# Fewer weight units split ahead at the norm boundaries of a two-layer encoder, and later loads for the first Strassen tile

## The chip, the cores and the metric

The kernel runs on one core of a Trainium2 chip. The metric is device time in microseconds (us) from one launch of the kernel; lower is better. The compute engines are TensorE (PE, with its weight loads shown as PEld), VectorE (DVE), ScalarE (ACT) and GpSimd (POOL). SyncE (SP) and POOL issue the transfers.

## The reference

Two sequences, one of 512 tokens (the prompt) and one of 256 (the sample), pass through two layers of a bidirectional encoder with 1024 features. Each layer has three parts, and each part ends in a layer norm:

```python
for l in range(DEPTH):                                   # DEPTH = 2
    mod = (silu(c) @ ada_w[l] + ada_b[l]).reshape(B, 9, D_MODEL)
    h = modulate(x, mod[:, 0], mod[:, 1])
    x = layer_norm(ALPHA * x + 0.5 * (1 + mod[:, 2]) * swiglu(h, ffn1_wi[l], ffn1_wo[l]), ...)
    h = modulate(x, mod[:, 3], mod[:, 4])
    o = concat([rms_norm(window_attention(h @ w_in)), rms_norm(hyena(h @ w_in))]) @ w_out[l]
    x = layer_norm(ALPHA * x + (1 + mod[:, 5]) * o, ...)
    h = modulate(x, mod[:, 6], mod[:, 7])
    x = layer_norm(ALPHA * x + 0.5 * (1 + mod[:, 8]) * swiglu(h, ffn2_wi[l], ffn2_wo[l]), ...)
```

`swiglu(h)` is `(silu(g) * u) @ wo` with `g, u = split(h @ wi)`; the inner width is 2816, 22 tiles of 128.

## The kernel before, in words

All 768 tokens are held with features on the partitions, so the activations are eight tiles of 128 features by 768 tokens (columns 0 to 511 are the prompt, 512 to 767 the sample). Every operand of a product is split into a high and a low part (type fp32r) and each product is three matmuls: high by high, high by low, low by high.

**Weight units.** Weights stand in DRAM as `w_units`, blocks of 128 by 1024 numbers (512 KB). A unit is loaded by SP into a raw buffer (`slot_r`, seven of them), then split: ACT copies it to the high half of a `slot_w` buffer (six of them), and DVE subtracts to make the low half. `w_ahead(n)` splits units, in the order in which they are used, until n are ready beyond those taken; `w_take()` hands out the next one; `w_load` issues the raw loads up to three units past the one just split. `w_state["limit"]` ends the run of units at the head of a feed-forward part, which has six of them.

**The order.** The schedule is written out by hand: every engine carries out its instructions in the order in which the Python code issues them, and waits on the data of others. So what stands earlier in the code on ACT or DVE delays what stands later on the same engine.

**A norm boundary.** `final` ends a part and begins the next one; there are five such boundaries (feed-forward to mixer, mixer to feed-forward, feed-forward to feed-forward, and again the first two in layer 1). It first does the sample's output products (`sample_out`). Then a loop over eight output tiles d does the prompt's products on PE, and beside it the layer norm of the sample: `norm.stats(1)`, `norm.bcast(1)`, and `norm.apply(1, i)`, which normalises one tile, modulates it and splits it into `hh` and `hl`, the inputs of the next part. Inside this loop, and once after it, `w_ahead` splits units for the next part. Then `proj.head` runs:

- for each of n_head units (six ahead of a feed-forward part, four ahead of a mixer) it takes the unit, calls `w_ahead`, does 24 matmuls of 256 sample columns, and calls `hook(i)`;
- `hook(0)` makes the statistics of the prompt (`norm.stats(0)`: eight PE transposes, DVE reductions, a power on POOL) and calls `proj.early()`;
- `hook(2)` broadcasts them (`norm.bcast(0)`, eight PE transposes) and issues `norm.apply(0, d)` for all eight prompt tiles in one go;
- after the units comes the prompt's loop: four units by eight input tiles by three matmuls of 512 columns, then `mid()`, the activations of those four, `late()`, and the last two units on the prompt.

Here the six units of the head are called u0 to u5. A unit's split has the form `slot_w<-slot_r 128x1024` in the profile, on ACT and on DVE.

**The first Strassen tile.** In a feed-forward part tiles 0 to 2 (six units) use the plain product, and the other 19 tiles use a Strassen product of seven half-size products (class `Fast`). The first of them, tile 3 (`NHEAD`), needs two raw units, loaded by `load(NHEAD, slot_r)`. Its sums and splits are made in `late()`. `mixed(d)` makes sums of activations for it on DVE and ACT. Four of the seven `slot_r` buffers hold joined activations (`full(d)` for d over 3) from the sample's `norm.apply` on until `mixed` is done.

Of the kernel before, what the change touches and what calls it, by code (L numbers as in the profile page):

```python
# [152 lines left out]
@with_exitstack  # L153
def encoder_kernel(ctx, tc, *args):
    ctx.enter_context(tc.manual_schedule())
    last = {}
    _program(_Memory(None, None, None, SLOTS, last), None, *args)
    _program(_Memory(tc.nc, tc, ctx, SLOTS, last), tc.nc, *args)


def _program(mem, nc, x_in, c_col, c_row, w_units, ada_nat, ada_t, ada_b, ln_p, conv_p, sink_in, grp_in,
# [4 lines left out]
    def slot_s(shape, dtype=F32):  # L166
        return mem.alloc("slot_s", shape, dtype)

    def slot_w(shape, dtype=F32R):
        return mem.alloc("slot_w", shape, dtype)  # L170
# [6 lines left out]
    def slot_t(shape, dtype=F32):  # L177
        return mem.alloc("slot_t", shape, dtype)
# [9 lines left out]
    def f32(ap):  # L188
        return ap.bitcast(F32)

    def tt(out, a, b, op, eng=vec):
        eng.tensor_tensor(out=out, in0=a, in1=b, op=op)
# [10 lines left out]
    def acopy(out, a):  # L203
        act.activation(out=out, in_=a, func=AF.Copy)
# [27 lines left out]
    n_units = len(w_order)  # L232
# [3 lines left out]
    def w_load(upto):  # L236
        while w_state["dma"] < min(upto, w_state["limit"]):
            i = w_state["dma"]
            w_raw[i] = slot_r([D])
            sp.dma_start(w_raw[i], w_units[w_order[i]])  # L240
            w_state["dma"] += 1

    def w_ahead(n):
        while w_state["split"] < min(w_state["next"] + n, w_state["limit"]):
            i = w_state["split"]
            w_load(i + 1)
            raw = w_raw.pop(i)
            w = slot_w([2, D])
            acopy(w[:, 0], raw)
            tt(w[:, 1], raw, f32(w[:, 0]), ALU.subtract)  # L250
            w_split[i] = w
            w_state["split"] += 1
            w_load(i + w_state["raws"])
# [13 lines left out]
    def pump(n):  # L267
        while n > 0 and background:
            try:
                next(background[0])  # L270
            except StopIteration:
                background.pop(0)
                continue
            n -= 1

    def drain():
        while background:
            pump(1)
# [35 lines left out]
    def split_to(hi, lo, src):  # L314
        acopy(hi, src)
        tt(lo, src, f32(hi), ALU.subtract)
# [88 lines left out]
    def coef_of(l, mod, c0):  # L405
        c = tiny([ND, 2])
        ts(c, mods[l][:, mod], c0, c0)
        return c
# [26 lines left out]
    class Proj:  # L435
# [15 lines left out]
            self.done(i, 0, bp[:, :LP])  # L451
            self.done(i, 1, bs[:, :LS])

        def early(self):
            pass

        mid = late = early

        def head(self, n, hook):

# [58 lines left out]
    def out_add(o, coef, d):  # L519

        bp, bs = bank(), bank()
        o.d([(bp[:, :LP], 0), (bs[:, :LS], 1)], d)
        v = slot_t([T])
        for s, b in ((0, bp[:, :LP]), (1, bs[:, :LS])):
            act.activation(out=v[:, SEQ[s]], in_=b, func=AF.Copy, scale=coef[:, d, s:s + 1])
        gp.dma_start(x_spill[:, d, :], v, accum_op=ALU.add)

    def sample_out(os, norm):

        for o in os:  # L530
            for i in range(4):
                if i in o.hooks:
                    o.hooks[i]()
                outs = []
                for j in range(2):
                    b, more = o.place(1, 2 * i + j, j == 1)
                    o.d([(b, 1)], 2 * i + j, more=more)
                    outs.append(b)
                for j in range(2):
                    if o is os[-1]:  # L540
                        norm.add(2 * i + j, 1, outs[j])
                    else:
                        norm.plain(2 * i + j, 1, outs[j])
                pump(1)
        drain()

    def final(os, norm, proj, n_head, spill):

        sample_out(os, norm)
        o = os[-1]  # L550
        n_units = sum(o.n for o in os)
        when = (0, 2, 3) if n_units > 4 else (1, 3, 4)
        for d in range(ND):
            bp, more = o.place(0, d)
            for i, part in enumerate(os):
                part.d([(bp, 0)], d, more=more or i > 0, less=part is not o)
            w_ahead(min(4, 6 - n_units + sum((d + 1) * part.n // 8 for part in os)))
            if d == when[0]:
                norm.stats(1)
            if d == when[1]:  # L560
                norm.bcast(1)
            for i in range(2 * (d - when[2]), 2 * (d - when[2]) + 2):
                if 0 <= i < ND:
                    norm.apply(1, i)
            norm.add(d, 0, bp)
        for i in range(2 * (ND - when[2]), ND):
            norm.apply(1, i)
        for j in range(2):
            spill(1, j)
        norm.low()  # L570
        norm.low()
        norm.squares()
        w_ahead(6)

        def hook(i):
            if i == 0:
                norm.stats(0)
            elif i == 2:
                norm.bcast(0)
                for d in range(ND):  # L580
                    norm.apply(0, d)
                    if d % 4 == 3:
                        spill(0, d // 4)
                norm.low()
                norm.low()
            if i == 0:
                proj.early()

        proj.head(n_head, hook)

    def results(os, norm):
# [24 lines left out]
    def swiglu(x, hh, hl, l, which):  # L616
        a_tiles, pend = {}, {}

        def a_of(j):
            if j // 2 not in a_tiles:  # L620
                a_tiles[j // 2] = slot_s([2, 2, T], F32R)
            return a_tiles[j // 2][:, j % 2]

        def done(i, s, ps):
            j, c = i // 2, SEQ[s]
            if i % 2 == 0:
                if (j, 0) not in pend and (j, 1) not in pend:
                    pend[j] = slot_t([T])
                act.activation(out=pend[j][:, c], in_=ps, func=AF.Silu)
                pend[(j, s)] = True  # L630
                return
            sg, a = pend[j], a_of(j)
            tt(sg[:, c], sg[:, c], ps, ALU.mult)
            pend[("d", j)] = pend.get(("d", j), 0) + 1
            split_to(a[:, 0, c], a[:, 1, c], sg[:, c])

        proj = Proj(hh, hl, done)
        fast = Fast(hh, hl, w_fast[2 * l + which // 2], a_of, which)
        proj.fast, proj.early, proj.mid, proj.late = fast, fast.early, fast.mid, fast.late

        def rest(end):
            coef = None
            os = []
            fast.begin()
            for ci, chunk in enumerate(CHUNKS):
                last = ci + 1 == len(CHUNKS)
                while fast.j < UNTIL[ci]:
                    fast.period(fast.j + 1 == UNTIL[ci])
                if coef is None:
                    coef = coef_of(l, 3 * which + 2, 0.5 / ALPHA)  # L650
                o = Out([(a_of(j)[:, 0], a_of(j)[:, 1]) for j in chunk])
                if ci + 2 >= len(CHUNKS):
                    if not os:
                        xn = Feat()
                        for i in range(2):
                            gp.dma_start(xn.more(i), x_spill[:, 4 * i:4 * i + 4, :])
                    o.room = 6 - sum(before.n for before in os)
                    os.append(o)
                    if last:
                        drain()  # L660
                        return end(os, xn, coef)
                    continue
                w_state["limit"], o.ahead = w_state["next"] + len(chunk), 1
                for d in range(ND):
                    out_add(o, coef, d)
                    pump(1)
                    if d % 2:
                        w_ahead(2)

        return proj, rest  # L670

    class Fast:
# [25 lines left out]
            al = slice(0, T)  # L698
            tt(self.full(d, al), f32(self.hh(d, al)), f32(self.hl(d, al)), ALU.add)

        def early(self):
            self.load(NHEAD, slot_r)

        def mid(self):
            for d in range(4):
                self.mixed(d)

# [458 lines left out]
    def first_h(d):  # L1166
        for c, s in ((SEQ[0], 0), (SEQ[1], 1)):
# [6 lines left out]
            tt(h[1](d, c), v, f32(h[0](d, c)), ALU.subtract, eng=vec if s else gp)  # L1174

    part = swiglu(x, *h, 0, 0)
    hs = [lambda d=d: first_h(d) for d in range(ND)]
    filt[1].spectra(0, sides(hs[0], hs[1], hs[2], skip, hs[3], skip, hs[4], skip))
# [581 lines left out]
    for i in range(len(PARTS)):  # L1760
# [5 lines left out]
        part = part[1](lambda os, xx, coef, i=i: finish(i, os, xx, coef))  # L1766
# [159 lines left out]
```

## Time and profile before

| | |
|---|---|
| median of 3 runs | 2939.13 us (2938.8 to 2939.33) |
| the profiled execution | 2938.19 us, span 2936.2 us |
| PE busy | 2837.5 us, 97% of the span |
| DVE, ACT, POOL busy | 2139.2 us, 1367.5 us, 331.8 us |
| mean granted TensorE clock | 0.987 |
| DMA, mean over the span | 124 GB/s |

The span runs from the first to the last instruction of the profiled execution; its own time is 1.99 us longer and 0.94 us under the median of the runs. PE is busy nearly all the time, so the time changes where PE idles or where its clock falls. A timeline row gives the start in us, the duration in us of the merged instructions, the engine, line (always that of a helper that records every call), operation, output and inputs by tile name, shapes, how many instructions were merged, and in brackets the idle time of that engine just before and what ended it.

### The profile page before, as it was taken

The page shows a single profiled execution, that of the slowest core. Times are in us where ns is not written, and L with a number is a line of the kernel's source. Part 1 is how long each engine was busy: PE and PEld are TensorE (multiplying, and loading weights), DVE is VectorE, ACT ScalarE, POOL GpSimd, SP SyncE. Part 2 cuts the span into 40 slices and gives each one's busy share as a digit, 9 for nine tenths or more (in the row PEclk, how much of TensorE's full clock was granted, in tenths as well). Part 3 has the DMA queues.
Part 4 walks back from the last instruction along what each step waited for, and adds up shares of the span by engine and source line. Part 5 has one row for each costly group of instructions (what it writes and reads, how often), then busy time and mean ns, then how long its engine had stood idle before and what let it go on. Part 6 is the DMA issues. An engine that isn't in the chain of part 4 may idle for free. (4 is left out here: it accounts for less than half of the span.)

```text
span 2936.2 us, 42164 instructions
## 1 busy us (share of the span) xinstructions
PE 2837.5 (97%) x16468; PEld 2594.4 (88%) x16468; DVE 2139.2 (73%) x3821; ACT 1367.5 (47%) x2355; POOL 331.8 (11%) x394
## 2 busy tenths in 40 slices
PE   9999999999998999999999999999999899999998
PEld 3789999988887889999988999998888788999997
DVE  5788778878967887777588777557896787444558
ACT  3544444444366544444445444444436644444444
POOL 2400000031000300000030000002100030000000
PEclk9999999999999999999999999999999999999999
DMA  5546665542121135664333665344212112455332
GB/s 202 194 171 173 188 176 164 147 151 103 57 73 51 65 127 161 194 194 116 107 122 122 179 176 157 107 107 145 102 63 73 51 57 89 85 115 115 97 108 83
DMA packets 102607, 364.65 MB, mean 124 GB/s; under 512 B 13750, under 2 KB 17031, under 8 KB 99208
## 3 DMA queue, kind: packets, MB, share of 16 engines
q1 hardware_dynamic: 74968, 259.88, 24.5%
q0 software_dynamic: 27440, 102.08, 16.2%
q8 instruction: 129, 2.11, 0.3%
q14 instruction: 70, 0.57, 0.1%
HBM read 284.33 MB, written 80.74 MB: 124 GB/s over the span
## 5 line engine op out<-in xcount | busy, mean ns | idle before, releaser
L70 PE MATMUL bank<-slot_s,slot_w 128*128 128x384 f32 (+2 forms) x13176 | 2322.1, 336 | 44.0 <-DVE slot_s L70 26.7
L70 PEld LDWEIGHTS bank<-slot_s,slot_w 128*128 128x128 f32 x13176 | 2130.5, 190 | 212.2 <-DVE slot_s L70 23.0
L70 DVE TENSOR_TENSOR slot_w<-slot_w,slot_w 128x1024 fp32r<-128x1024 f32 (+2 forms) x444 | 370.0, 864 | 4.1 <-ACT slot_w L70 1.6
L70 DVE CUSTOM_DVE_ANT_0 slot_t<-slot_r,slot_r 128x1024 bf16<-128x1024 f32 x256 | 311.4, 1223 | 77.4 <-DMA x_spill<-slot_t 45.0
L70 ACT ACTIVATE slot_w<-slot_w 128x1024 fp32r<-128x1024 f32 (+1 forms) x298 | 249.7, 838 | 119.2 <-DVE slot_w L70 118.9
L70 DVE TENSOR_TENSOR slot_w<-slot_r,slot_w 128x1024 fp32r<-128x1024 f32 (+1 forms) x194 | 222.0, 1153 | 113.4 <-ACT slot_w L70 111.9
L70 ACT ACTIVATE slot_t<-bank,tiny 128x512 f32<-128x512 f32 (+1 forms) x256 | 147.5, 580 | 307.9 <-PE bank L70 302.1
L70 POOL DMA_DIRECT2D x_spill<-slot_t x128 | 110.4, 862 | 1409.2 <-ACT slot_t L70 1409.2
L70 ACT ACTIVATE slot_w<-slot_r 128x1024 fp32r<-128x1024 f32 (+1 forms) x194 | 189.0, 992 | 155.9 <-DVE slot_r L70 98.1
L70 ACT ACTIVATE slot_t<-slot_t 128x384 f32<-128x384 f32 (+2 forms) x161 | 84.1, 526 | 334.2 <-DVE slot_t L70 334.0
L70 DVE TENSOR_TENSOR slot_t<-bank,slot_t 128x384 f32<-128x384 f32 x228 | 125.5, 555 | 144.2 <-PE bank L70 73.5
L70 DVE TENSOR_TENSOR slot_s<-slot_t,slot_s 128x768 fp32r<-128x768 f32 (+2 forms) x190 | 153.1, 810 | 52.6 <-ACT slot_s L70 48.4
L70 ACT ACTIVATE slot_s<-slot_t 128x768 fp32r<-128x768 f32 (+2 forms) x160 | 113.8, 717 | 159.9 <-DVE slot_t L70 155.5
L70 ACT ACTIVATE slot_t<-bank 128x384 f32<-128x384 f32 (+3 forms) x282 | 139.6, 495 | 101.6 <-PE bank L70 99.1
L70 PE MATMUL bank<-slot_s,slot_r 128*128 128x384 f32 x912 | 172.0, 337 | 0.0
L70 PEld LDWEIGHTS bank<-slot_s,slot_r 128*128 128x128 f32 x912 | 160.6, 188 | 0.0
L70 DVE TENSOR_TENSOR slot_r<-slot_w,slot_r 128x512 fp32r<-128x512 f32 x76 | 52.0, 684 | 106.4 <-ACT slot_r L70 106.4
L70 ACT ACTIVATE slot_t<-slot_s 128x256 f32<-128x256 f32 (+1 forms) x132 | 65.9, 510 | 108.0 <-DVE slot_s L70 104.1
L70 PE MATMUL bank<-slot_w,slot_s 128*128 128x256 f32 x864 | 107.9, 284 | 3.1 <-DVE slot_w L70 1.8
L70 PEld LDWEIGHTS bank<-slot_w,slot_s 128*128 128x128 f32 x864 | 104.7, 191 | 3.9 <-DVE slot_w L70 2.1
L70 DVE SCALAR_TENSOR_TENSOR slot_t<-bank,slot_t 128x384 f32<-128x384 f32 x76 | 42.3, 556 | 83.4 <-PE bank L70 82.2
L70 DVE SCALAR_TENSOR_TENSOR slot_s<-bank,tiny,slot_s 128x256 f32<-128x256 f32 (+1 forms) x160 | 87.0, 564 | 15.1 <-PE bank L70 14.9
(137 smaller groups left out, 2132.2 us busy)
## 6 DMA issues: line engine op xcount, KB each, us to landing
slot_r<-w_units SPq DMA_DIRECT2D x170, 512.0 KB, 4.8
slot_w<-w_units SPq DMA_DIRECT2D x146, 512.0 KB, 4.1
slot_r<-ada_t SPq DMA_DIRECT2D x128, 512.0 KB, 5.8
x_spill<-slot_t POOLq DMA_DIRECT2D x128, 384.0 KB, 5.3
slot_s<-x_spill POOLq DMA_DIRECT2D x12, 1536.0 KB, 8.2
x_spill<-slot_s POOLq DMA_DIRECT2D x10, 1024.0 KB, 4.6
slot_r<-ada_nat SPq DMA_DIRECT2D x16, 512.0 KB, 5.9
g_main<-slot_s POOLq DMA_DIRECT2D x4, 1536.0 KB, 10.0
```

The lines of the kernel that those rows point to most:

```text
L70: return getattr(real, name)(*args, **kwargs)
```

## The change

Inside the loop of `final` at most two units are split ahead instead of four, and the call after the loop also asks for two instead of six. `hook(0)` no longer calls `early`; the loads that `early` issued now stand at the start of `mid`, after the prompt's loop.

```diff
@@ class Proj
-        def early(self):
+        def mid(self):
             pass
 
-        mid = late = early
+        late = mid
@@ final
-            w_ahead(min(4, 6 - n_units + sum((d + 1) * part.n // 8 for part in os)))
+            w_ahead(min(2, 6 - n_units + sum((d + 1) * part.n // 8 for part in os)))
...
         norm.squares()
-        w_ahead(6)
+        w_ahead(2)
@@ hook in final
-            if i == 0:
-                proj.early()
-
@@ swiglu
-        proj.fast, proj.early, proj.mid, proj.late = fast, fast.early, fast.mid, fast.late
+        proj.fast, proj.mid, proj.late = fast, fast.mid, fast.late
@@ class Fast
-        def early(self):
+        def mid(self):
             self.load(NHEAD, slot_r)
-
-        def mid(self):
             for d in range(4):
                 self.mixed(d)
```

The calls in `Proj.head` stay as they are: `w_ahead(min(2, 6 - len(ws)))` after each `w_take()`.

## Rows read from the trace of the kernel before

**Rows 1.** The page, busy time of each engine, share of the span, instructions.

```profile
PE 2837.5 (97%) x16468; PEld 2594.4 (88%) x16468; DVE 2139.2 (73%) x3821; ACT 1367.5 (47%) x2355; POOL 331.8 (11%) x394
```

**Rows 2.** Windows: start:end, length, busy us (instructions) by engine, PEclk, DMA share, GB/s.

```profile
960.00:1050.00 90.00, 84.15 (x456) 72.92 (x456) 76.71 (x136) 45.15 (x72) 30.68 (x33) 0.94 0.16 59
1050.00:1470.00 420.00, 416.75 (x2371) 397.09 (x2370) 310.33 (x470) 184.90 (x296) 28.70 (x34) 1.00 0.54 154
```

**Rows 3.** Timeline of PE, boundary from mixer to feed-forward, layer 0.

```profile
983.67 11.98 PE L70 MATMUL bank<-slot_s,slot_w 128*128 128x512 f32 x55
...
1000.06 2.00 PE L70 MATMUL bank<-slot_s,slot_w 128*128 128x256 f32 x6 [2.39 <-DVE slot_s L70]
1004.07 1.44 PE L70 MATMUL bank<-slot_s,slot_w 128*128 128x256 f32 x5 [2.00 <-DVE slot_s L70]
1005.31 1.91 PE L70 MATMUL bank<-ident,slot_t 128*128 128x128 f32 x8
1006.87 6.96 PE L70 MATMUL bank<-slot_s,slot_w 128*128 128x256 f32 x48
...
1014.46 46.06 PE L70 MATMUL bank<-slot_s,slot_w 128*128 128x256 f32 x240
1062.23 13.02 PE L70 MATMUL bank<-slot_s,slot_w 128*128 128x384 f32 x71 [1.71 <-ACT slot_t L70]
```

**Rows 4.** Timeline of DVE, the same boundary.

```profile
984.61 1.75 DVE L70 TENSOR_TENSOR slot_w<-slot_r,slot_w 128x1024 fp32r<-128x1024 f32 x1 [0.49 <-ACT slot_w L70]
...
1004.87 2.35 DVE L70 TENSOR_TENSOR slot_w<-slot_r,slot_w 128x1024 fp32r<-128x1024 f32 x2
...
1012.77 0.42 DVE L70 TENSOR_TENSOR slot_t<-slot_t,bank 128x256 f32<-128x256 f32 x1 [3.67 <-ACT slot_t L70]
...
1014.37 0.69 DVE L70 TENSOR_TENSOR slot_t<-slot_s,bank 128x512 f32<-128x512 f32 x1 [0.28 <-PE bank L70]
...
1031.24 0.69 DVE L70 TENSOR_TENSOR slot_s<-slot_r,slot_s 128x512 fp32r<-128x512 f32 x1 [0.99 <-ACT slot_r L70]
```

**Rows 5.** Timeline of ACT, the same boundary.

```profile
1002.89 1.99 ACT L70 ACTIVATE slot_w<-slot_r 128x1024 fp32r<-128x1024 f32 x2
...
1030.40 0.80 ACT L70 ACTIVATE slot_r<-slot_t,tiny,tiny 128x512 f32<-128x512 f32 x1
...
1051.41 1.05 ACT L70 ACTIVATE slot_w<-slot_r 128x1024 fp32r<-128x1024 f32 x1
```

**Rows 6.** Timeline of PE, boundary from feed-forward to feed-forward.

```profile
1504.14 22.94 PE L70 MATMUL bank<-slot_s,slot_w 128*128 128x512 f32 x109
...
1528.14 0.86 PE L70 MATMUL bank<-slot_s,slot_w 128*128 128x256 f32 x5 [1.05 <-DVE slot_s L70]
...
1529.63 6.00 PE L70 MATMUL bank<-slot_s,slot_w 128*128 128x256 f32 x48
...
1536.25 45.74 PE L70 MATMUL bank<-slot_s,slot_w 128*128 128x256 f32 x240
```

**Rows 7.** Timeline of DVE, the same boundary as rows 6.

```profile
1515.30 2.36 DVE L70 TENSOR_TENSOR slot_w<-slot_r,slot_w 128x1024 fp32r<-128x1024 f32 x2 [1.33 <-ACT slot_w L70]
...
1536.10 0.69 DVE L70 TENSOR_TENSOR slot_t<-slot_s,bank 128x512 f32<-128x512 f32 x1 [1.48 <-PE bank L70]
```

**Rows 8.** Timeline of PE, boundary from feed-forward to mixer, layer 0.

```profile
653.77 1.17 PE L70 MATMUL bank<-slot_s,slot_w 128*128 128x256 f32 x5 [2.03 <-DVE slot_s L70]
...
656.30 6.54 PE L70 MATMUL bank<-slot_s,slot_w 128*128 128x256 f32 x48
...
667.65 22.52 PE L70 MATMUL bank<-slot_s,slot_w 128*128 128x512 f32 x98 [0.83 <-DVE slot_s L70]
```

**Rows 9.** Windows inside the boundary of rows 3, for the granted clock.

```profile
1006.00:1008.00 2.00, 2.00 (x11) 2.00 (x10) 2.00 (x4) 0.00 (x0) 0.00 (x0) 0.50 0.96 260
...
1010.00:1012.00 2.00, 2.00 (x19) 2.00 (x19) 0.00 (x0) 0.94 (x1) 0.41 (x2) 1.00 0.76 291
```

**Rows 10.** DMA issues: output, input, queue, count, KB each, median us to landing.

```profile
slot_r<-w_units SPq DMA_DIRECT2D x170, 512.0 KB, 4.8
```

## What the change is predicted to do

> **What bounds the kernel now.** I read the page first: PE is busy 97% of the span [rows 1], so only PE's idle time, about 99 us, and its clock can move. The windows say where that idle time is: 5.85 of 90 us at a norm boundary, against 3.25 of 420 us in the feed-forward part behind it, and the granted clock is lower there too [rows 2]. Then I read the boundary on PE, DVE and ACT side by side [rows 3 to 5]. The prompt's output products end near 995 (983.67 plus 48 of them at the 0.23 us of rows 8), u0 advances in pieces because `hl` of the sample's norm is late on DVE, and its last five matmuls start at 1004.07. DVE is late partly because it also splits units: one inside that stretch (1.75 us after a wait of 0.49) and two at its end (2.35 us) [rows 4]. At the boundary between two feed-forward parts the same wait is 1.05 us [rows 6], at the one into the mixer 2.03 us [rows 8]; layer 1 repeats the patterns of rows 3 and 8 once each, within 0.15 us. From the start of u3 on, PE runs without a gap for 46 us, 240 matmuls [rows 3, 6]: u3 to u5, the prompt's loop, the last two units and the first two Strassen products. In that stretch DVE and ACT work through the eight prompt tiles of `norm.apply(0, d)`, from 1014.37 to 1031.93 on DVE and to 1031.20 on ACT [rows 4, 5], unseen by PE. That cover is what to watch.
>
> **The change part by part. The new order of the splits.** Read `head` with two units split on entry. Taking u0 splits u2; taking u1 splits u3, behind `stats(0)`; taking u2 splits u4, just ahead of `hook(2)`. `hook(2)` then issues all eight tiles to DVE, ACT and POOL. Only after that does taking u3 split u5. So ahead of a feed-forward part the sixth unit's split stands behind the whole apply on both in-order queues, while PE wants u5 before the prompt's loop; everything behind u5 on PE waits as well. Ahead of a mixer there are four units; u0 to u3 are all split before `hook(2)`, and what falls behind it (u5 again, there the second unit after the head) is wanted only after a prompt loop of 22.5 us [rows 8].
>
> **Term A, the wait for u5, three boundaries.** Before, u5 starts once u3 and u4 are through: 48 such matmuls take 6.00 us [rows 6], so 6.1 us after the first apply. After, the last ACT instruction of the apply ends 16.8 us after the first apply (1030.40 + 0.80 - 1014.37), ACT's copy of u5 adds 1.0 (half of 1.99) and DVE's subtraction 1.2 (half of 2.35) [rows 4, 5]: u5 is ready after 19.0 us. The wait is 19.0 - 6.1 = 12.9 us, less what the apply starts earlier.
>
> How much earlier? From mixer to feed-forward DVE loses the 1.75 and the wait of 0.49, and a split just before that sat mostly in a wait, so the sample's last `hl` comes some 2.7 us earlier (2.2 to 3.0). Behind it stand one split instead of two, the statistics, u1 and u2 on PE, then u3's split, the activations of u0 and u1 and u4's split, which use the hole of 3.67 us that DVE has there [rows 4]. u4's split ends last, about 1012.5, where the apply starts at 1014.37 now: 1.9 us earlier; the ends are 1.0 (the activations wait for a PE that still runs slowly) and 2.8 (all the gain passes). From feed-forward to feed-forward the two splits inside the loop go (2.36 after a wait of 1.33 [rows 7]), but the last output tile comes from PE only about 1524.8 (1504.14 plus 90 products of 0.23 us [rows 6, 8]), so `hl` gains about half a us and u4's split takes most of it back: 0.2 us, ends 0 and 0.6. The sum: 2 x (12.9 - 1.9) + (12.9 - 0.2) = 34.7 us; ends 32.5 and 36.7.
>
> **Term B, the clock.** In the boundary of rows 3 the granted clock stands at 0.50, the 1.2 GHz level, when PE resumes after its pieces of idle time, and is back at 1.00, 2.4 GHz, in 1010 to 1012 [rows 9]. From the last matmuls of u0 to the start of u3 the same 69 instructions (5 matmuls, 8 transposes, 48 matmuls, 8 transposes) take 10.39 us (1004.07 to 1014.46) against 8.11 us (1528.14 to 1536.25) where the wait was short and the clock full [rows 3, 6]: 2.28 us. Into the mixer it is 9.07 against 7.49 (to the end of the 48), 1.58 us [rows 6, 8]. A wait of 12 us is longer than any of these, so u5 and the start of the prompt's loop should run slowly once at each of the three: 2.28 each, 6.8 us. The lower end is 0 (a wait of 1.05 us cost nothing), the upper 3.5 each, 10.5, half as much again for a longer wait.
>
> **Term C, the boundaries into the mixer.** Two splits leave the loop, and `hl` is then tied to PE's last tile: of the 2.03 us of idle time I take 1.25, and the slow stretch of 1.58 should go with the rest, since 1.05 us left the clock alone [rows 6, 8]. 2.8 us each, 5.6 us gained; ends 2.5 (the clock still falls) and 8.9 for both (all the idle time, the slow stretch and the wait of 0.83 go). u5's split now follows the apply; the prompt's loop hides it, and bare it would cost 1.2 us each.
>
> **Term D, the end of the head.** Between the second Strassen product and the third PE waits 1.71 us for ACT [rows 3]. With `mixed` done long before a later prompt loop, DVE can take the activations at once; I give 0.5 us each, 1.5 gained; ends 0 and 5.1.
>
> **The loads moved to `mid`.** Two loads at each of three boundaries leave their place behind `hook(0)` on SP and pass the loads of u4 and u5, which the later splits bring with them; the condition rows for the background modulation work queue behind them at two boundaries. SP waits only for free raw buffers: four of seven hold joined activations, and the two that the moved loads get were those of u3 and u4, free once u4 is split, near 1013. A load lands in 4.8 us [rows 10], two by about 1023; ACT wants the first at 1051.41 [rows 5], and 12 us later after the change. So I cost the move at nothing. The Trainium skill, in Trainium Kernel Development and Optimization, section Best Practices, advises to double-buffer so that transfers overlap compute, and a load moved behind the work that covered it speaks against this change: by that reading one load of 4.8 us would be bare at each of three boundaries and the sum would be 14 us higher. The rows of this case show 28 us of room instead. No matmul is added or removed, nor any split; POOL's spill queue is not passed.
>
> **Sum.** 34.7 + 6.8 - 5.6 - 1.5 = 34.4 us. Against the profiled execution, 2938.19 + 34.4 = 2972.6; that execution is 0.94 us under the median, so the median should become 2973.5 us, 1.2% slower.
>
> **The rivals. Faster: the splits fit the hole.** If u5's split came through ahead of the apply, only the earlier starts would be left: 1.9 + 1.9 + 0.2 + 5.6 + 1.5 = 11 us gained, 2928 us. The waits of PE for DVE [rows 3, 8] speak for it, and so does the hole of 3.67 us, which three splits of 1.2 us would just fit. It decides by whether u5's split is issued before or after the eight applies, and `head` issues it after. 4 in 100.
>
> **No change: the wait takes the place of another.** If PE had to wait for the apply in the prompt's loop anyway, u5's wait would only come earlier, and with the gains the time would stay near 2939 us. It needs some 12 us of idle time behind u3, and PE's 240 matmuls there show none [rows 3, 6]. 3 in 100.
>
> **Slower still: the late loads are bare.** If SP issued them only when PE has left the prompt's loop, `late` would wait 4.8 us for one load or 9.6 for two at each of three boundaries: 2988 to 3002 us. The buffers' order speaks against it. 6 in 100.
>
> **How the numbers follow.** The forecast has 87 in 100. Its ends: 32.5 + 0 - 8.9 - 5.1 = 18.5 and 36.7 + 10.5 - 2.5 = 44.7, so 2957.6 to 2983.8; not all terms fall on one side together, so I give 2959 to 2983. About 0.2%, 5.9 us, is what a measurement can tell from no change. Forecast and late loads are slower, 93 in 100; same 3, faster 4.
>
> **What would show it.** Right: at three boundaries PE idles about 11 to 13 us waiting for DVE `slot_w`, between 48 matmuls and the rest of the former 240, with a granted clock near 0.5 behind it; one split on DVE and ACT stands right behind the last apply; the wait for `slot_s` at u0 shrinks by some 2 us; ACT's first split in `late` shows no wait for DMA. Wrong: no gap after u4; or the gap's releaser is a DMA; or DVE waits for a raw unit in `late`; or the boundaries into the mixer grow too.

## The result and the profile after

The changed kernel takes 2969.76 us (median of 4 runs, 2967.02 to 2970.46) against 2938.97 us (4 runs, 2938.65 to 2939.33): 1.0108 times as long, 95% interval 1.0095 to 1.0122. Its profiled execution is its shortest, 2967.02 us with a span of 2964.9 us, 28.7 us more than the span before.

The busy times have not changed: the page's line answers to [rows 1] within 4 us on every engine. PE's busy time, in which matmuls at the slow clock count at their full length, differs by 0.1 us: slow stretches that went and slow stretches that came balance, and nearly all of the 28.7 us is idle time of PE.

```profile
PE 2837.6 (96%) x16468; PEld 2596.1 (88%) x16468; DVE 2140.1 (72%) x3821; ACT 1367.8 (46%) x2355; POOL 335.7 (11%) x394
```

The timeline of PE in the changed kernel shows where: the boundary into the mixer in layer 0 answers to [rows 8], the one from mixer to feed-forward to [rows 3], the one between two feed-forward parts to [rows 6].

```profile
651.12 0.86 PE L70 MATMUL bank<-slot_s,slot_w 128*128 128x256 f32 x5 [0.60 <-DVE slot_s L70]
...
663.40 28.82 PE L70 MATMUL bank<-slot_s,slot_w 128*128 128x512 f32 x132 [0.82 <-DVE slot_s L70]
...
999.15 1.44 PE L70 MATMUL bank<-slot_s,slot_w 128*128 128x256 f32 x5 [2.18 <-DVE slot_s L70]
...
1009.11 5.99 PE L70 MATMUL bank<-slot_s,slot_w 128*128 128x256 f32 x48
1028.23 0.79 PE L70 MATMUL bank<-slot_s,slot_w 128*128 128x256 f32 x2 [13.12 <-ACT slot_w L70]
1029.49 54.84 PE L70 MATMUL bank<-slot_s,slot_w 128*128 128x256 f32 x262 [0.46 <-DVE slot_w L70]
1084.16 2.28 PE L70 MATMUL bank<-slot_s,slot_r 128*128 128x384 f32 x12
...
1544.76 6.00 PE L70 MATMUL bank<-slot_s,slot_w 128*128 128x256 f32 x48
1562.60 0.80 PE L70 MATMUL bank<-slot_s,slot_w 128*128 128x256 f32 x2 [11.84 <-ACT slot_w L70]
1563.86 53.56 PE L70 MATMUL bank<-slot_s,slot_w 128*128 128x256 f32 x262 [0.46 <-DVE slot_w L70]
```

What was one run of 240 matmuls is cut behind u3 and u4 (48 matmuls): PE stands still for 13.12 us, runs two matmuls, waits another 0.46 us, and goes on. The third feed-forward boundary shows 13.11 and 0.46 us. The wait of 1.71 us that stood before the third Strassen product [rows 3] is gone: the 262 matmuls run through. At the boundary into the mixer the wait for `slot_s` has shrunk from 2.03 to 0.60 us; from mixer to feed-forward the last of u0's waits is still 2.18 us (2.00 before).

DVE in the changed kernel, at the boundary of [rows 4]:

```profile
999.95 1.21 DVE L70 TENSOR_TENSOR slot_w<-slot_r,slot_w 128x1024 fp32r<-128x1024 f32 x1
...
1003.61 1.23 DVE L70 TENSOR_TENSOR slot_w<-slot_r,slot_w 128x1024 fp32r<-128x1024 f32 x1
...
1009.27 1.23 DVE L70 TENSOR_TENSOR slot_w<-slot_r,slot_w 128x1024 fp32r<-128x1024 f32 x1 [0.52 <-ACT slot_w L70]
1010.42 0.68 DVE L70 TENSOR_TENSOR slot_t<-slot_s,bank 128x512 f32<-128x512 f32 x1
...
1028.21 1.22 DVE L70 TENSOR_TENSOR slot_w<-slot_r,slot_w 128x1024 fp32r<-128x1024 f32 x1 [0.26 <-ACT slot_w L70]
...
1055.17 0.69 DVE L70 TENSOR_TENSOR slot_t<-slot_t,bank 128x512 f32<-128x512 f32 x1 [5.13 <-PE bank L70]
```

The four splits in order are those of u2, u3, u4 and, 19 us later, u5: the eight prompt tiles lie between the last two. ACT in the changed kernel copies u5 right behind its last tile, and the first split of `late` has no wait for a transfer, as in [rows 5]:

```profile
1027.13 1.04 ACT L70 ACTIVATE slot_w<-slot_r 128x1024 fp32r<-128x1024 f32 x1
...
1058.41 1.05 ACT L70 ACTIVATE slot_w<-slot_r 128x1024 fp32r<-128x1024 f32 x1
```

Windows of the changed kernel behind the three waits (columns as in [rows 2]), answering to [rows 9]: behind the first the granted clock is at 0.50, the 1.2 GHz level, when u5 starts, and back at 1.00, 2.4 GHz, some 6 us later. The last two rows show it at 0.50 behind the other two waits.

```profile
1028.00:1030.00 2.00, 1.31 (x4) 1.01 (x5) 1.56 (x2) 0.64 (x3) 0.09 (x1) 0.50 0.67 258
1030.00:1032.00 2.00, 2.00 (x11) 2.00 (x10) 0.43 (x1) 0.21 (x1) 0.00 (x0) 0.50 1.06 342
...
1034.00:1035.00 1.00, 1.00 (x7) 0.86 (x7) 0.13 (x1) 0.39 (x1) 0.00 (x0) 1.00 0.00 0
...
1564.00:1566.00 2.00, 2.00 (x10) 2.00 (x11) 0.56 (x2) 0.42 (x1) 0.00 (x0) 0.50 1.05 348
...
2446.00:2448.00 2.00, 2.00 (x9) 2.00 (x10) 0.68 (x2) 0.42 (x1) 0.00 (x0) 0.50 0.95 360
```

### The profile page after: what moved, and what is told of

The parts are those of the page before. It is cut to its first block, busy times and chain, and to the rows that moved or that the text cites. A ratio compares the mean times of both kernels' runs of the same rounds, so it can differ in the third digit from the quotient of the medians.

```text
span 2964.9 us, 42160 instructions
## 1 busy us (share of the span) xinstructions
PE 2837.6 (96%) x16468; PEld 2596.1 (88%) x16468; DVE 2140.1 (72%) x3821; ACT 1367.8 (46%) x2355; POOL 335.7 (11%) x394
## 5 line engine op out<-in xcount | busy, mean ns | idle before, releaser
L70 PE MATMUL bank<-slot_s,slot_w 128*128 128x384 f32 (+2 forms) x13176 | 2323.3, 336 | 71.5 <-ACT slot_w L70 38.1
L70 PEld LDWEIGHTS bank<-slot_s,slot_w 128*128 128x128 f32 x13176 | 2133.5, 190 | 237.9 <-ACT slot_w L70 38.7
```

The source lines that it names most:

```text
L70: return getattr(real, name)(*args, **kwargs)
```

## Experiments

The theory was that the place of u5's split, behind `norm.apply(0, d)`, makes the loss. The first rival was that splitting just in time is too late as such, the second that the moved loads are bare. All ratios are to the kernel before, run beside it on the same chip, with 95% intervals. A trace is one execution; two traces of kernels that do the same work up to the first boundary differ there by up to 3.7 us (`before` and `filled`, the start of the first statistics), so steps are read inside a boundary and not from the span.

**u5's split ahead of the apply** (`sixth_first`), from the changed kernel:

```diff
-                    w_ahead(min(2, 6 - len(ws)))
+                    w_ahead(min(3 if len(ws) == 3 else 2, 6 - len(ws)))
```

> The changed kernel with one difference: when u2 is taken, u5 is split as well as u4, so its split is issued ahead of the prompt's apply. If the loss comes from the place of u5's split in the order (the theory), the waits of 12 to 13 us at the three feed-forward boundaries go, and the earlier sample stays: about 2.9 us gained at each mixer boundary, 2.9 at each boundary from mixer to feed-forward and 0.4 between two feed-forward parts, 12 us in all, 2927 us. If splitting just in time is too late as such (first rival), u3 and u4 still come late and most of the loss stays: 2950 to 2970 us. If the loads moved to mid are the loss (second rival), nothing changes: about 2970 us.

Measured: 2941.06 us, 1.0011 (1.0003 to 1.0020). The loss is gone but for 3 us, which speaks for the theory; but the 12 us of gain did not come, a miss by 14 us. PE in this run:

```profile
1009.65 46.06 PE L70 MATMUL bank<-slot_s,slot_w 128*128 128x256 f32 x240
1059.93 15.30 PE L70 MATMUL bank<-slot_s,slot_w 128*128 128x384 f32 x72 [4.22 <-ACT slot_t L70]
...
1586.03 13.22 PE L70 MATMUL bank<-slot_s,slot_w 128*128 128x384 f32 x72 [3.55 <-ACT slot_t L70]
```

The 240 matmuls run in one piece again and start 4.8 us sooner than in [rows 3], but the wait at their end is 4.22 us instead of 1.71, and the 72 matmuls behind it take 15.30 us where such 72 take 13.22 at the full clock: the gain is given back at the end of the head. It is more than given back: from the sample's broadcast (the four transposes ahead of each boundary's waits) to the first product on `slot_r`, the three feed-forward boundaries take 1.9, 1.2 and 1.6 us longer than in the kernel before, which eats the 2.4 and 2.3 us that the two boundaries into the mixer gain here. There, too, the edit puts u5's split ahead of the apply, and the wait at the start of the prompt's loop is 1.43 us instead of 0.83. What holds PE at the end of the head was the next question (below).

**Only the loads moved** (`load_late`), from the kernel before: `load(NHEAD, slot_r)` from `early` to the start of `mid`.

> The kernel before with only the two raw loads of the first Strassen tile moved from hook(0) to mid, all splits as before. Theory: SP does not wait for PE but only for free raw buffers, so the loads still land some 25 us before they are wanted: 2939 us, within 2. Rival, the late loads are bare: one or two loads of 4.8 us at each of three boundaries, 2953 to 2968 us.

Measured: 2938.52 us, 0.9998 (0.9989 to 1.0007). The moved loads cost nothing, and the second rival falls. ACT reaches `late` there without a wait for a transfer:

```profile
1047.96 1.05 ACT L70 ACTIVATE slot_w<-slot_r 128x1024 fp32r<-128x1024 f32 x1
```

This run shows one thing more. At the boundary into the mixer PE waits as before, but the transposes and matmuls behind the wait run at the full clock (in [rows 8] the 48 matmuls take 6.54 us):

```profile
651.45 0.87 PE L70 MATMUL bank<-slot_s,slot_w 128*128 128x256 f32 x5 [1.96 <-DVE slot_s L70]
652.15 1.04 PE L70 MATMUL bank<-ident,slot_t 128*128 128x128 f32 x8
652.95 5.99 PE L70 MATMUL bank<-slot_s,slot_w 128*128 128x256 f32 x48
```

So a wait of this length lowers the clock in some executions and not in others. Of the four kernels that keep the long wait (1.90 to 2.03 us; the kernel before, this one, `sixth_late` and `before_light` below), six of eight such boundaries show the slow stretch; of the nine with a wait of 0.60 to 0.65 us, none of 18.

**Only u5 late** (`sixth_late`), from the kernel before:

```diff
-        w_ahead(6)
+        w_ahead(6 if n_head == 4 else 5)
```

> The kernel before with one number changed, at the feed-forward boundaries alone: five units instead of six after the loop, so only u5 is left to be split behind the apply; the loop still splits four and the loads stay at hook(0). Theory: the whole loss is there and none of the gain. The wait is about 17.9 - 6.1 = 11.8 us each (u5's first matmuls need only ACT's half), with 2 us of slow clock and 0.5 us for DVE's half, less the 1.7 to 2.0 us wait at the end of the head that goes: 3 x 12.4 = 37 us, 2976 us. First rival (too few units ahead in general): five of six are ready, so at most a sixth of the loss, 2944 us. Second rival (late loads): 2939 us.

Measured: 2971.59 us, 1.0115 (1.0101 to 1.0129). One unit of six, at three places, brings the whole loss (33.6 us), while all others are ready early; the first rival falls. PE's three waits are 11.74, 11.66 and 11.74 us where 11.8 was expected; the time is 4 us under the expectation. The middle one:

```profile
1566.87 0.79 PE L70 MATMUL bank<-slot_s,slot_w 128*128 128x256 f32 x2 [11.66 <-ACT slot_w L70]
```

**Only the boundaries into the mixer** (`mixer_only`), from the kernel before:

```diff
-            w_ahead(min(4, 6 - n_units + ...))
+            w_ahead(min(2 if n_head == 4 else 4, 6 - n_units + ...))
...
-        w_ahead(6)
+        w_ahead(2 if n_head == 4 else 6)
```

> The kernel before with the limit of two units only at the two boundaries into the mixer (four head units, no load moved). Theory: these two gain, 2.8 to 3.0 us each, 2933 us. Rival, fewer units ahead cost at every boundary: 2939 us or more.

Measured: 2934.6 us, 0.9987 (0.9978 to 0.9996): of the versions that leave nothing out, the only one that comes out ahead of both kernels, by 0.13%, which is less than the 0.2% that the prediction asks of a clear difference. In its trace PE's wait for `slot_s` is 0.60 us and the eight transposes behind it run at the full clock; inside the two boundaries PE gains 3.02 and 2.85 us on the kernel before:

```profile
649.39 0.86 PE L70 MATMUL bank<-slot_s,slot_w 128*128 128x256 f32 x5 [0.60 <-DVE slot_s L70]
650.09 1.03 PE L70 MATMUL bank<-ident,slot_t 128*128 128x128 f32 x8
```

**u5's split behind four of eight tiles** (`sixth_mid`), from the changed kernel, inside the loop of `hook(2)`:

```diff
                     norm.apply(0, d)
+                    if d == 3:
+                        w_ahead(3)
```

> The changed kernel with u5's split issued inside hook(2), behind four of the eight prompt tiles instead of behind all. If u5's place sets the loss, each tile passed is worth 2.07 us of DVE time, so the waits of 13.1, 11.8 and 13.1 us fall by 8.3 each and with them the time by about 25 us, to 2945 us. There DVE's own chain through the head is nearly the bound (the run with u5 ahead of the apply gave 2941), so it cannot be under 2941. If only being behind the whole of hook(2) counted, it would stay near 2970.

Measured: 2948.74 us, 1.0039 (1.0027 to 1.0050). Half the tiles, a third of the loss: the waits are 4.81, 3.53 and 4.80 us, each 8.3 less than in the changed kernel, as 2.07 us for each tile says. The time is 3.7 us over the expectation. At the two boundaries into the mixer, too, the edit puts u5's split between the tiles, and PE gets a new wait in the prompt's loop there, 2.15 and 2.07 us. The rows are from the first boundary into the mixer and the first into a feed-forward part.

```profile
671.00 33.07 PE L70 MATMUL bank<-slot_s,slot_w 128*128 128x512 f32 x167 [2.15 <-DVE slot_s L70]
...
1021.30 0.80 PE L70 MATMUL bank<-slot_s,slot_w 128*128 128x256 f32 x2 [4.81 <-ACT slot_w L70]
```

**The wait filled with matmuls** (`filled`), from the changed kernel, ahead of u5:

```diff
+                    if len(ws) == 6:
+                        idle = bank()
+                        for _ in range(12):
+                            for k in range(ND):
+                                mm(idle[:, :LS], blk(ws[4], 0, k), self.hh(k, SEQ[1]), k == 0, k == ND - 1)
```

> The changed kernel with 96 extra matmuls of 256 columns on PE between u4 and u5 of each feed-forward head, into a bank that nothing reads (extra work, about 11.7 us, nothing left out). They fill the wait for u5, so u5 starts as before the filling but at the full clock. If the slow clock behind the wait costs 2.4, 1.4 and 2.2 us, as the rows of the changed kernel say, 6 us come back: 2964 us, a ratio of 1.0088 to the kernel before. If the slow clock is hidden behind DVE, which is the next bound, nothing comes back: 1.0108, 2970 us.

Measured: 2963.89 us, 1.0092 (1.0079 to 1.0105). PE does 11.5 us more work at each of three places and the kernel is not longer than the changed one; by the two ratios it is some 5 us shorter. The intervals of the two ratios overlap, so the trace has to carry it: from u5's start to the first 12 matmuls on `slot_r` this run takes 55.40, 53.57 and 53.59 us, the changed kernel 55.93, 54.66 and 55.52. The idle time that the filling leaves ahead of u5 is 1.62, 0.34 and 1.61 us. At the second and third place the clock stays full; at the first it fell once more, so 1.6 us of idle time goes with either level here. PE at the first place, then a window of the first and of the third place:

```profile
1005.31 17.51 PE L70 MATMUL bank<-slot_s,slot_w 128*128 128x256 f32 x144
1024.44 0.50 PE L70 MATMUL bank<-slot_s,slot_w 128*128 128x256 f32 x2 [1.62 <-ACT slot_w L70]
```

```profile
1026.00:1030.00 4.00, 4.00 (x23) 4.00 (x22) 0.42 (x1) 0.42 (x1) 0.00 (x0) 0.59 0.88 284
...
2446.00:2448.00 2.00, 2.00 (x17) 1.90 (x17) 0.00 (x0) 0.22 (x1) 0.00 (x0) 1.00 0.33 123
```

**What holds PE at the end of the head.** In `sixth_first` DVE works from the start of u3 to that wait with hardly a gap (44.9 of 50.3 us busy, no gap over 1 us). If its chain (the prompt's apply, `mixed`, the activations, the splits of `late`) is the second bound, a shorter chain should move the time where PE is early and not where PE is late. Two tries. First, one of `mixed`'s subtractions put on POOL:

```diff
-            tt(t4[:, 1], fb[:, 0], f32(t4[:, 0]), ALU.subtract)
+            tt(t4[:, 1], fb[:, 0], f32(t4[:, 0]), ALU.subtract, eng=gp)
```

> The kernel before with the limit of two units at the boundaries into the mixer alone, and with the last subtraction of mixed (the low part of t4, 0.55 us on DVE, four of them ahead of each first Strassen tile) on POOL instead of DVE. If DVE's chain is the second bound of the feed-forward heads (the wait of 1.7 to 2.0 us at their end), taking 2.2 us off it gives 1.7 us at each of three heads on top of the gain at the mixer boundaries: 2929 us, 0.997. If that wait comes from elsewhere, or POOL slows DVE by as much, as with the mixer boundaries alone: 2934 us, 0.9987.

> The changed kernel with the same subtraction of mixed on POOL. There PE is late by the wait for u5 and DVE idles 5 us ahead of the first activation, so a shorter DVE chain should be worth nothing: 2970 us, 1.0108. If DVE bound the head here too, 2965 us or less.

Measured: `mixer_pool` 2936.38 us, 0.9998 (0.9989 to 1.0006), a miss; `after_pool` 2967.99 us, 1.0103 (1.0090 to 1.0116). DVE's chain had not become shorter. POOL's subtraction takes 1.41 us, and the DVE instruction that overlaps it, the first of the next call of `mixed`, takes 1.37 us instead of 0.55. So the calls follow each other 3.81 us apart on DVE, against 3.46 in `mixer_only`, and the wait at the end of the head grew to 2.29 us, from 1.73 there. POOL, DVE and PE of `mixer_pool`:

```profile
1035.15 1.41 POOL L70 TENSOR_TENSOR slot_s<-slot_r,slot_s 128x384 fp32r<-128x384 f32 x1 [4.79 <-ACT slot_s L70]
```

```profile
1035.62 1.37 DVE L70 TENSOR_TENSOR slot_t<-slot_r,slot_s 128x384 f32<-128x384 f32 x1
...
1039.43 1.37 DVE L70 TENSOR_TENSOR slot_t<-slot_r,slot_s 128x384 f32<-128x384 f32 x1
```

```profile
1061.11 14.19 PE L70 MATMUL bank<-slot_s,slot_w 128*128 128x384 f32 x71 [2.29 <-ACT slot_t L70]
```

Second, the subtraction left out, with a copy on ACT in its place, in three kernels:

```diff
-            tt(t4[:, 1], fb[:, 0], f32(t4[:, 0]), ALU.subtract)
+            acopy(t4[:, 1], fb[:, 0])
```

> The run with u5 ahead of the apply, with the low part of t4 in mixed written by a copy on ACT instead of DVE's subtraction (the low part's value is changed, which leaves 0.55 us of DVE work out, four times per head). If DVE's chain through the head took the gain back there, as its waits of 4.2, 3.6 and 4.4 us at the end of the head say, these fall by 1.9 each, and the slow clock behind them may go too: 2931 to 2935 us, ratios 0.998 to 0.9995 against 1.0011 without it. If the waits have another cause, 1.0011.

> The kernel before with the same part of mixed left out. If the wait of 1.7 to 2.0 us at the end of each head is DVE's chain there as well, it goes at three heads: 2933 us, ratio 0.998. If not, 1.000.

> The changed kernel with the same part of mixed left out. PE is late there by the wait for u5 and has no wait at the end of the head, so the shorter DVE chain is worth nothing: ratio 1.0108, as without it. If DVE still bound the head, 1.009.

Measured: `sixth_light` 0.9989 (0.9980 to 0.9998) against 1.0011 without the edit; `before_light` 0.9975 (0.9966 to 0.9984) against 1; `after_light` 1.0109 (1.0095 to 1.0123) against 1.0108. So 2 us less on DVE is worth 6 to 7 us by the ratios where PE is early, and nothing where PE waits for u5. The waits at the first head's end fell from 1.71 to 0.24 us and from 4.22 to 2.75 us. Over the three heads the traces show 4.5 us for `before_light` (1.47, 1.49 and 1.50 of wait) and 3.9 for `sixth_light` (3.1 of wait, the rest slow clock), where waits shorter by 1.9 each were expected; where the rest of the ratios' gain lies they do not show. PE of `before_light`, then of `sixth_light`:

```profile
1058.24 13.22 PE L70 MATMUL bank<-slot_s,slot_w 128*128 128x384 f32 x72 [0.24 <-ACT slot_t L70]
```

```profile
1057.53 14.37 PE L70 MATMUL bank<-slot_s,slot_w 128*128 128x384 f32 x72 [2.75 <-ACT slot_t L70]
```

## Why the prediction was right, and where its terms were off

Measured +30.8 us by the medians and +28.7 us by the two spans; forecast +34.4, 2973.5 us, within 4 us of the median and inside the range. The start of the same instruction in both traces gives the account by steps. The line "broadcast" is the start of the four transposes that broadcast the sample's statistics, ahead of all waits of the boundary. The line u5 of each feed-forward boundary is its first matmul (before: the start of u3 plus the 6.00 us of [rows 6]), the last line the first 12 matmuls on `slot_r` weights.

```
                                              before    after difference
into the mixer, layer 0: broadcast            628.11   626.88     -1.23
    prompt's loop                             667.65   663.40     -4.25
mixer to feed-forward, layer 0: broadcast     983.32   980.87     -2.45
    u0's last                                1004.07   999.15     -4.92
    u3                                       1014.46  1009.11     -5.35
    u5                                       1020.46  1028.23     +7.77
    first product on slot_r                  1075.27  1084.16     +8.89
feed-forward to feed-forward: broadcast      1503.79  1512.74     +8.95
    u0's last                                1528.14  1536.65     +8.51
    u3                                       1536.25  1544.76     +8.51
    u5                                       1542.25  1562.60    +20.35
    first product on slot_r                  1597.00  1617.26    +20.26
into the mixer, layer 1: broadcast           2024.10  2045.34    +21.24
    prompt's loop                            2063.11  2081.50    +18.39
mixer to feed-forward, layer 1: broadcast    2379.10  2397.32    +18.22
    u3                                       2410.36  2425.61    +15.25
    u5                                       2416.36  2444.72    +28.36
    first product on slot_r                  2471.22  2500.24    +29.02
```

**Term A, the wait for u5.** Right in place and in size, the size partly by luck. Forecast were waits of 12.9 us each, 38.7, reduced by an earlier apply; the waits are 13.12, 11.84 and 13.11, 38.1 us. Two errors inside it cancel. The releaser was named wrongly: u5's first two matmuls take only the high half, so PE starts on ACT's copy, 1.2 us before DVE's subtraction ends, and then waits 0.46 us for that. And at the first place PE wants u5 4.7 us after the first apply (1009.11 + 6.00 - 1010.42) where the forecast had 6.1. That the split is ready 19.0 us after the first apply came out as forecast (1028.21 + 1.22 - 1010.42). `sixth_late`, `sixth_mid` and `sixth_first` show that the place of this one split makes the wait: behind eight tiles the whole loss, behind four a third, ahead of them next to none.

**Term B, the clock.** Forecast 6.8 us. From u5 to the first product on `slot_r` the three differences change by +1.12, -0.09 and +0.66, 1.7 us, though 5.7 us of waits at the end of the head (1.71, 1.98 and 2.05) have gone: 7.4 us went into this stretch, 1.4 of it the waits of 0.46 and the rest, 6.0 us, the slow clock. `filled` brought back 3.5 us of it in its trace, with the clock still falling at one of three places.

**Term C and the earlier apply.** Forecast were 5.6 us at the boundaries into the mixer and 4.0 at the others, 9.6 together. From the broadcast to the prompt's loop or to u3 the differences fall by 3.02 and 2.85 us into the mixer (forecast 2.8 each), by 2.90 and 2.97 from mixer to feed-forward (forecast 1.9 each) and by 0.44 between two feed-forward parts (forecast 0.2): 12.2 us. So Term C was right, and the earlier start of the others was put 2.3 us too low. Of the two gains into the mixer 1.43 and 1.26 us are idle time and 1.6 each the clock; that second share depends on the execution, as `load_late` shows. `mixer_only` shows the same 3.02 and 2.85 in its trace and 3.4 us in all by its medians, between 1.2 and 6.5 by its interval.

The differences also move between the boundaries, where the two kernels do the same work: by -1.23 us ahead of the first, +1.80 in layer 0's mixer, +0.98 in the first feed-forward part of layer 1. In that mixer `after_pool` and `after_light`, with the changed order of splits, lose 0.16 and 0.53 us against the kernel before, so this is taken as a difference between executions and not as the change's.

**Term D, the end of the head.** This is the term that was mis-sized most: 1.5 us, measured 5.7. I saw that DVE would be ready sooner relative to PE, but gave 0.5 of 1.7 us to each; the whole wait went, because PE came 12 us later and DVE then idled 5.13 us ahead of the first activation.

**The sum.** By steps the change costs 38.1 + 7.4 - 12.2 - 5.7 = 27.6 us, where the forecast had 34.4: the two gains, of the earlier starts and at the end of the head, were put 6.8 us too low together, while the two losses were right. The 30.8 us of the medians lie between, so part of the forecast's nearness to the median is luck.

**The loads** cost nothing, as forecast (`load_late`). In the changed kernel SP issued the last of them at 1010.53 us, where u4's split ends (1009.27 + 1.23), 47.9 us before ACT takes the first unit at 1058.41.

**The rivals.** The faster one had the right edit and the wrong price: with u5's split ahead of the apply the kernel comes to 1.0011, not to 2928 us. The 11 us took each earlier start as a gain to the end of the head. From mixer to feed-forward and between feed-forward parts that is not so: the splits taken out ahead of the head come back on DVE inside it, and PE waits for DVE at its end instead (`sixth_first`, and with less DVE work `sixth_light`). That these gains did count in the changed kernel is because the wait for u5 left DVE time to spare, which `after_light` bears out. The two other rivals are excluded by `sixth_late` and `load_late`.

Left open: `mixed`'s first call, in the first feed-forward part, is also touched by the last three kernels, and its share of their gain was not measured by itself. Why a wait of 1.6 to 2.0 us is followed by the slow clock in one execution and not in another is not shown either.

## What to carry to other kernels

When splits or loads are handed out "n ahead", follow each one to its place in the in-order queue of the engine that does it, and look for the longest block of other work that can come in front: here lowering the depth cost 3 us as long as all six splits were issued ahead of a block of eight tiles (`sixth_first`), and 34 us when a single one fell behind it (`sixth_late`). Time taken off an engine early in a stage is a gain only if the work does not come back on the same engine before the stage's next wait for it; price both paths to the end of the stage. A deeper queue of ready weights can be cut where the next block leaves room (the boundaries into the mixer, though the gain was only 0.13% here) and kept where it doesn't.

## What the hardware showed that I had not expected

- A subtraction of 128 by 384 numbers on POOL took 1.41 to 1.44 us at the three heads, and the DVE instruction of the same size that ran beside it took 1.37 us instead of 0.55: moving 0.55 us from DVE to POOL made DVE's chain longer, not shorter. In the first head the fourth ran beside a DVE instruction of 128 by 512 that reads a PSUM bank, and that one kept its 0.68 us.
- Giving PE 11.5 us of useless matmuls in each of three waits did not make the kernel longer, and probably a little shorter than leaving PE idle (1.0092 against 1.0108, with overlapping intervals; 3.5 us in the traces): the granted clock stayed at 1.00 behind two of the three waits.
- Waits of the same length left the clock alone or lowered it: 1.61 us left it at 1.00 and 1.62 us was followed by 0.59 in the same trace (`filled`), and 1.90 us did either in two kernels (`load_late` and the kernel before).
